# A hybrid-heads decoder layer: small vectors asked for by GpSimd, x scaled on ScalarE in halves, and 14 and 13 pairs visited in the second and third groups

## The chip, the cores and the metric

The kernel runs on one core of one Trainium2 chip. The metric is the device time of one execution in microseconds (us). Three timed runs of the kernel before are known, and one further execution of it was taken with the hardware profiler; all rows below come from that one.

The engines are named as the profile names them: PE is TensorE's matmul, PEld its weight load, DVE is VectorE, ACT is ScalarE, POOL is GpSimd, SP is SyncE, whose queue (SPq) issues the transfers of this kernel.

## What is computed

One decoder layer over 256 tokens and 2048 columns, all in float32. The parts that matter here are the first half: a modulated RMSNorm, one wide projection, and four token mixers that share it.

```python
mod = (cond @ w_mod[l] + b_mod[l]).reshape(B, 6, D)          # cond = silu(c)
sh1, sc1, g1, sh2, sc2, g2 = [mod[:, i, None, :] for i in range(6)]
h = rmsnorm(x, norm_mix[l]) * (1.0 + sc1) + sh1
proj = f32(h @ w_in[l])                                      # 2048 x 5660
y_a = gla_mixer(...)            # needs gla_w_lr, gla_b_lr, gla_norm
y_b = gated_deltanet_mixer(...) # needs gdn_conv, gdn_a_log, gdn_dt_bias, gdn_norm
y_c = pool_mixer(...)           # needs pool_w, pool_scale
y_d = forgetting_attention(...) # needs fox_f_bias
x = x + g1 * (concat(y_a, y_b, y_c, y_d) @ w_out[l])
h = rmsnorm(x, norm_ffn[l]) * (1.0 + sc2) + sh2
x = x + g2 * conv_ffn(h, ...)
```

## The kernel before

**Products in three parts.** Each weight piece (a tile `wr`, 512 KB, loaded by SP) is split into a rounded part `wh` (a cast on ACT, line 115) and a rest `wl` (a subtraction on DVE, line 100), and each product is three matmuls: high by high, high by low, low by high. One loaded piece of `w_in` feeds 24 matmuls of 256 columns. `wr` has 5 buffers, `wh` and `wl` have 3 each.

**Four groups.** The 16 blocks of 128 input columns are taken in four groups of four (`GROUPS`, line 46). For each group, `mods(g)` computes the shift and scale of its columns as a vector product on DVE: 16 tiles `wm` of 512 KB are loaded and added into `ga` one after the other (`accumulate`, lines 168 to 172; `wm` has 5 buffers there). The function `f` inside `mods4` (lines 342 to 354) then folds `ga` with eight tiny matmuls against `ones`, makes `md`, scales the normalized and transposed x (`xnT`, stored in `bigC`) into `h`, and splits `h` into the matmul operand `HL` (stored in `bigA`). Before the first group, x is loaded (`xt`), its squares are summed, GpSimd raises the sum to the power -1/2 (line 320), x is scaled row by row (lines 321 and 322), and 32 transposes on PE with copies on ACT make `xnT`.

**What a group computes.** In stage g, `gdn(g)` (lines 410 to 424) adds the group's part of the DeltaNet's query, key and value into six PSUM tiles `acc` that stay open over all groups: 6 pieces, 144 matmuls. Then `extras(g)` (lines 470 to 474) visits some of the 16 *pairs* of 128-column tiles that make up the rest of the projection (`pairs`, in `ORDER` "gpfd": 6 for GLA, 2 for pooling, 6 for the forgetting attention, 2 for the DeltaNet's gate). A visit (`pair`, lines 438 to 459) multiplies all groups that this pair has not had yet, one piece and 24 matmuls for each, and adds the PSUM tile `ext` into its place (`pr`, `gv` or `fv`). `TAKE` (line 49) says how many pairs stage 0, 1 and 2 visit, counted from the end of the list; the last stage visits all 16. While a stage runs, the loads and additions of the next group's `wm` are interleaved with it (`next(nxt, None)`).

**Small vectors.** `rest()` (lines 367 to 393) loads thirteen small things (the low-rank weights, convolution weights, norms, biases, the constants `ct`), transposes three of them on PE, copies them on ACT, and makes twelve masks `mk` on GpSimd. `small_load()` (lines 396 to 400) loads 28 columns of `w_in` into `wsm` by three transfers of 16, 8 and 4 columns, that is 2048 pieces of 64, 32 and 16 bytes, and splits them into `wsh` (ACT) and `wsl` (DVE). Both are called after the third piece of `gdn(0)`. `small()` multiplies with them at the start of stage 3, and `gates()` follows.

**The last stage and the mixers.** After `gdn(3)`, the accumulators are copied and convolved, and `gated_deltanet()` runs as a long chain of small steps on PE (tiles `gdt`), DVE and ACT. PE fills its gaps with the pairs still to visit (`ext`), with GLA, pooling and forgetting attention (`oxt`), and with the vector products for the second half (`bgt` on PE, more `ga` on DVE). The output projection (`project`, lines 950 to 968, first into `ext`, then into `wot`) follows.

**What sets the order.** A planner orders each engine's instructions by the time at which it expects them to be ready, and by their place in the code where several are. On the chip every engine and every queue then runs its list strictly in that order: an instruction whose input is late holds up all that stand behind it on its engine. `tc.issue_after(x)` puts the instructions of a block behind `x` on the engine of `x`.

Of the kernel before, what the change touches and what calls it, by code (L numbers as in the profile page):

```python
# [11 lines left out]
AF = mybir.ActivationFunctionType  # L12
ALU = mybir.AluOpType
# [32 lines left out]
GROUPS = ((0, 4), (4, 4), (8, 4), (12, 4))  # L46
NG = len(GROUPS)

TAKE = (16, 12, 11)

ORDER = "gpfd"

# [21 lines left out]
def trunk_kernel(ctx: ExitStack, tc: tile.TileContext, x, c, w_mod, b_mod, norm_mix, norm_ffn, w_in,  # L74
# [24 lines left out]
    def tt(o, a, b, op):  # L99
        V.tensor_tensor(out=o, in0=a, in1=b, op=op)  # L100
# [4 lines left out]
    def tsc(o, a, s1, s2, op0, op1=None):  # L105
        if op1 is None:
            V.tensor_scalar(out=o, in0=a, scalar1=s1, scalar2=None, op0=op0)
        else:
            V.tensor_scalar(out=o, in0=a, scalar1=s1, scalar2=s2, op0=op0, op1=op1)

    def act(o, a, f, **kw):
        S_.activation(o, a, f, **kw)

    def split(hi, lo, src):
        S_.copy(hi, src)  # L115
        tt(lo, src, hi.bitcast(F32), ALU.subtract)
# [111 lines left out]
    with ExitStack() as ph:  # L228
# [59 lines left out]
        with ExitStack() as st:  # L288
# [29 lines left out]
                act(flat(pr[:, 0:8]), xt[:, t], AF.Square, accum_out=ssm[:, t:t + 1])  # L318
            tsc(ssm[:, 2:4], ssm[:, 0:2], 1.0 / D, EPS, ALU.mult, ALU.add)
            G.tensor_tensor(out=ssm[:, 0:2], in0=ssm[:, 2:4], in1=mhalf[:, 0:2], op=ALU.pow)  # L320
            for t in range(NT):
                tsc(xt[:, t], xt[:, t], ssm[:, t:t + 1], None, ALU.mult)
            for k in range(0, KT, 2):
                b = ext().rearrange("p (k t) -> p k t", t=T)
                for kk in range(2):
# [9 lines left out]
            def mods(g):  # L335
                for k0 in range(GROUPS[g][0], sum(GROUPS[g]), 4):
                    yield from mods4(k0, min(4, sum(GROUPS[g]) - k0))

            def mods4(k0, nk):
                n = nk * P  # L340

                def f(ga):
                    b = ext()
                    for i in range(2 * nk):
                        mm(b[:, i:i + 1], ga[:, i * P:i * P + P], ones[:, 0:1])
                    md = sp.tile([P, 2 * nk], F32, name="md", tag="md", bufs=2, padded_shape=[P, 16])
                    tt(md[:, 0:nk], b[:, 0:nk], bm(0, k0, nk), ALU.add)
                    tt(md[:, nk:], b[:, nk:2 * nk], bm(1, k0, nk), ALU.add)
                    tt(md[:, nk:], md[:, nk:], nmix[:, k0:k0 + nk], ALU.mult)
                    for kk in range(nk):  # L350
                        k = k0 + kk
                        h = sp.tile([P, T], F32, name="h", tag="h", bufs=2)
                        act(h, xnT[:, k], AF.Identity, scale=md[:, nk + kk:nk + kk + 1], bias=md[:, kk:kk + 1])
                        split(HL[:, k, 0:T], HL[:, k, T:], h)
                views = [wm_v[:, k, 0:2 * D].rearrange("p (s n) -> p s n", n=D)[:, :, P * k0:P * k0 + n]
                         for k in range(KT)]
                ga = keep.tile([P, 2 * n], F32, name="ga", tag="ga", padded_shape=[P, 1024])
                for k in range(KT):
                    wm = sp.tile([P, 2 * n], F32, name="wm", tag="wm", bufs=5, padded_shape=[P, 1024])
                    last_wm[0] = nc.sync.dma_start(wm.rearrange("p (s n) -> p s n", n=n), views[k])  # L360
                    accumulate(ga, wm, k)
                    if k == KT - 1:
                        with tc.high_priority():
                            f(ga)
                    yield

            def rest():
                nc.sync.dma_start(wlr[0:16], gla_w_lr[0])
                nc.sync.dma_start(wlr[28:29], gla_b_lr)
                nc.sync.dma_start(r2[0:48], gdn_conv[0].rearrange("j (k p) -> (j k) p", p=P))  # L370
                nc.sync.dma_start(r2[48:52], pool_scale[0].rearrange("(k p) -> k p", p=P))
                nc.sync.dma_start(r2[52:53], gla_norm)
                nc.sync.dma_start(r2[53:54], gdn_norm)
                nc.sync.dma_start(ct, cst[:, P:K_N])
                row = lambda ap: ap.partition_broadcast(P).rearrange("p o h -> p (o h)")
                nc.sync.dma_start(hrow[:, 0:4], row(gdn_a_log))
                nc.sync.dma_start(hrow[:, 4:8], row(gdn_dt_bias))
                nc.sync.dma_start(hrow[:, 8:12], row(fox_f_bias))
                nc.sync.dma_start(r3, ffn_conv_w[0, 0:2].rearrange("j (k p) -> (j k) p", p=P))
                nc.sync.dma_start(r4[0:NF], ffn_conv_w[0, 2].rearrange("(k p) -> k p", p=P))  # L380
                nc.sync.dma_start(r4[NF:], ffn_conv_b[0].rearrange("(k p) -> k p", p=P))
                b = ext()
                PE.transpose(b[:, 0:54], r2, ident[0:54, 0:54])
                S_.copy(V2, b[:, 0:54])
                b = ext()
                PE.transpose(b[:, 0:2 * NF], r3, ident[:2 * NF, :2 * NF])
                PE.transpose(b[:, 2 * NF:4 * NF], r4, ident[:2 * NF, :2 * NF])
                S_.copy(V3, b[:, 0:3 * NF])
                S_.copy(CB, b[:, 3 * NF:4 * NF])
                S_.copy(idr, ident)  # L390
                S_.copy(ngr, K(K_NEG))
                for i, m_ in enumerate(up + lw):
                    G.tensor_scalar(out=m_, in0=K(K_LV), scalar1=float(i + 1), scalar2=None, op0=ALU.is_equal)


            def small_load():
                nc.sync.dma_start(wsm[:, :, 0:16], wi_v[:, :, C_LR:C_LR + 16])
                nc.sync.dma_start(wsm[:, :, 16:24], wi_v[:, :, C_B:C_B + 8])
                nc.sync.dma_start(wsm[:, :, 24:28], wi_v[:, :, C_FF:C_FF + 4])  # L399
                split(wsh, wsl, wsm)  # L400

            def small():
                o = ext()[0:28, 0:T]
                for k in range(KT):
                    mm(o, wsh[:, k], HL[:, k, 0:T], start=k == 0, stop=False)
                    mm(o, wsh[:, k], HL[:, k, T:], start=False, stop=False)
                    mm(o, wsl[:, k], HL[:, k, 0:T], start=False, stop=k == KT - 1)
                S_.copy(smT[0:28], o)
# [101 lines left out]
            for g in range(NG):  # L510
                nxt = mods(g + 1) if g < NG - 1 else iter(())
                with tc.issue_after(hold[0].ins):
                    if g == NG - 1:
                        small()
                        gates()
                    for i, _ in enumerate(gdn(g)):
                        next(nxt, None)
                        if g == 0 and i == 2:
                            rest()
                            small_load()  # L520
                    if g == NG - 1:
                        break
                    for _ in extras(g):
                        next(nxt, None)
                for _ in nxt:
                    pass
                hold[0] = last_wm[0]


            qc = bigC()  # L530
# [600 lines left out]
```

## Time and profile before

| | us |
|---|---|
| median of 3 runs | 1305.72 (1299.94 to 1308.62) |
| the profiled execution | 1303.01 |
| its span from first to last instruction | 1301.2 |
| PE busy in it | 1248.5 (96%) |
| DVE busy | 891.0 (68%) |
| ACT busy | 636.7 (49%) |

The page of the profile cuts the span into 40 slices of 32.5 us. Busy PE time there does not mean full speed: matmuls overlap, so a stretch is better judged by how many matmuls it held and by the clock that TensorE was granted (PEclk, 1.00 for 2.4 GHz, 0.50 for 1.2 GHz).

### The profile page before, as it was taken

The numbers are of one execution on the slowest core, as the hardware profiler recorded it, in microseconds if no ns is written. First come the engines' busy times: TensorE is split into PE (matmuls) and PEld (weight loads), VectorE is DVE, ScalarE is ACT, GpSimd is POOL, SyncE is SP. The second block draws the span as 40 slices with busy tenths as digits, with TensorE's granted clock in tenths as the row PEclk, the third lists the DMA queues.
The fourth block names the chain that finished last, engine by engine and source line by source line (L and its number), as shares of the span: only waits on it lengthen the run. The fifth ranks groups of instructions, "written<-read, shape, count | busy, mean of one in ns | idle before, by whom it ended". The sixth has DMA issues, their size and how long they took to land.

```text
span 1301.2 us, 20372 instructions
## 1 busy us (share of the span) xinstructions
PE 1248.5 (96%) x7927; PEld 1091.0 (84%) x7927; DVE 891.0 (68%) x1201; ACT 636.7 (49%) x1000; POOL 22.7 (2%) x31
## 2 busy tenths in 40 slices
PE   2799999999999999999999999999999999999996
PEld 1799999898876788888888888888888888888896
DVE  7689797989763397676656656665656597964543
ACT  3455344774354454564545555554555454443432
POOL 0200000010000100000000000000000000000000
PEclk9799999999999999999999999999999999999998
DMA  9999998796566988556576666666665699875652
GB/s 321 277 367 378 337 341 290 259 339 212 164 236 240 318 317 276 156 165 192 163 214 190 186 187 193 190 172 206 187 187 163 219 374 359 323 243 194 192 181 81
DMA packets 174231, 311.94 MB, mean 240 GB/s; under 512 B 16172, under 2 KB 65331, under 8 KB 173495
## 3 DMA queue, kind: packets, MB, share of 16 engines
q1 hardware_dynamic: 174135, 310.65, 72.9%
q8 instruction: 62, 1.02, 0.3%
q14 instruction: 34, 0.28, 0.1%
HBM read 308.51 MB, written 2.10 MB: 239 GB/s over the span
## 4 chain that ended last, share of the span: by engine, by line
PE 92%; DMA 4%; SPq 1%; DVE 1%; ACT 1%; issue 1%; POOLq 0%; ACTq 0%; DVEq 0%
PE fpt L97 57%; PE ext L97 16%; PE wot L97 5%; PE gdt L97 4%; PE acc L97 4%; PE bgt L97 3%; DMA wm<-in_w_mod_dram 3%; PE oxt L97 2%; DMA wr<-in_w_in_dram 1%; DVE ga L103 1%; DMA ct<-in_cst_dram 0%; ACT xT L1011 0%; DVE wl L100 0%; SPq L399 0%; SPq L155 0%
## 5 line engine op out<-in xcount | busy, mean ns | idle before, releaser
L100 DVE TENSOR_TENSOR wl<-wr,wh 128x1024 fp32r<-128x1024 f32 x384 | 469.2, 1223 | 293.6 <-ACT wh L115 292.6
L115 ACT CAST wh<-wr 128x1024 fp32r<-128x1024 f32 x384 | 403.4, 1051 | 494.9 <-PE fpt L97 310.8
L97 PE MATMUL fpt<-bigA,wh 128*128 128x512 f32 x1408 | 399.6, 395 | 2.1 <-DVE bigA L103 2.1
L97 PEld LDWEIGHTS fpt<-bigA,wh 128*128 128x128 f32 x1408 | 239.3, 189 | 32.8 <-issue 2.2
L97 PEld LDWEIGHTS fpt<-bigA,wl 128*128 128x128 f32 x1408 | 222.4, 188 | 34.4 <-DVE wl L100 3.6
L97 PE MATMUL fpt<-bigA,wl 128*128 128x256 f32 x1408 | 240.4, 279 | 0.0
L103 DVE SCALAR_TENSOR_TENSOR ga<-wm,cond,ga 128x1024 f32<-128x1024 f32 x139 | 177.8, 1279 | 9.5 <-DMA wm<-in_w_mod_dram 8.6
L97 PE MATMUL fpt<-wl,AH 128*128 128x512 f32 (+1 forms) x440 | 152.9, 348 | 0.0
L97 PE MATMUL fpt<-wh,AL 128*128 128x512 f32 (+1 forms) x440 | 152.5, 347 | 0.0
L97 PE MATMUL fpt<-wh,AH 128*128 128x512 f32 (+1 forms) x440 | 142.5, 348 | 0.0
L97 PE MATMUL ext<-bigA,wh 128*128 128x256 f32 x768 | 137.0, 280 | 0.0
L97 PEld LDWEIGHTS ext<-bigA,wh 128*128 128x128 f32 x768 | 117.3, 188 | 3.1 <-DVE dS L100 0.8
L97 PE MATMUL ext<-bigA,wl 128*128 128x256 f32 x384 | 107.2, 280 | 1.7 <-DVE wl L100 1.7
L97 PEld LDWEIGHTS fpt<-wh,AH 128*128 128x128 f32 x440 | 83.3, 189 | 10.7 <-issue 0.2
L97 PEld LDWEIGHTS fpt<-wh,AL 128*128 128x128 f32 x440 | 83.3, 189 | 10.5 <-issue 0.2
L97 PEld LDWEIGHTS fpt<-wl,AH 128*128 128x128 f32 x440 | 83.3, 189 | 10.5 <-issue 0.2
L97 PE MATMUL acc<-bigA,wh 128*128 128x256 f32 x384 | 70.3, 289 | 4.7 <-ACT bigA L115 2.9
L97 PEld LDWEIGHTS ext<-bigA,wl 128*128 128x128 f32 x384 | 72.1, 188 | 3.0 <-DVE wl L100 2.1
L97 PE MATMUL ext<-wh,bigA 128*128 128x256 f32 (+1 forms) x320 | 68.0, 304 | 0.0
L97 PEld LDWEIGHTS acc<-bigA,wh 128*128 128x128 f32 x384 | 60.7, 198 | 5.1 <-ACT bigA L115 3.0
L97 PE MATMUL wot<-wh,bigA 128*128 128x512 f32 (+1 forms) x256 | 63.2, 337 | 0.0
L97 PEld LDWEIGHTS ext<-wh,bigA 128*128 128x128 f32 x320 | 51.7, 188 | 5.5 <-ACT wh L115 1.7
(340 smaller groups left out, 1191.9 us busy)
## 6 DMA issues: line engine op xcount, KB each, us to landing
wm<-in_w_mod_dram SPq DMA_DIRECT2D x192, 512.0 KB, 5.8
wr<-in_w_in_dram SPq DMA_DIRECT2D x88, 512.0 KB, 9.7
wr<-in_ffn_w_gate_dram SPq DMA_DIRECT2D x88, 512.0 KB, 3.9
wr<-in_ffn_w_up_dram SPq DMA_DIRECT2D x88, 512.0 KB, 4.4
wr<-in_ffn_w_down_dram SPq DMA_DIRECT2D x88, 512.0 KB, 4.5
wr<-in_w_out_dram SPq DMA_DIRECT2D x32, 512.0 KB, 4.2
xt<-in_x_dram SPq DMA_DIRECT2D x2, 1024.0 KB, 7.2
bigC<-in_x_dram SPq DMA_DIRECT2D x2, 1024.0 KB, 8.6
```

Of the source, the lines that this page charges most:

```text
L97: PE.matmul(o, lhsT=l, rhs=r, start=start, stop=stop, skip_group_check=True)
L100: V.tensor_tensor(out=o, in0=a, in1=b, op=op)
L103: V.scalar_tensor_tensor(out=o, in0=a, scalar=s, in1=b, op0=op0, op1=op1)
L115: S_.copy(hi, src)
```

## The change

Four edits. (1) x is scaled on ACT instead of DVE, in two halves of 1024 columns for each of the two row tiles. (2) The thirteen small transfers and the three of `wsm` are issued by GpSimd instead of SP. They stand behind a multiplication that GpSimd now does for group 1 (`asked`), `wsm` first. (3) The work on them moves back: `rest()` (transposes, copies, masks) is called after stage 2, and the split of `wsm` stands in `small()`. (4) `TAKE` is (16, 14, 13) instead of (16, 12, 11).

```diff
-TAKE = (16, 12, 11)
+TAKE = (16, 14, 13)
...
-            for t in range(NT):
-                tsc(xt[:, t], xt[:, t], ssm[:, t:t + 1], None, ALU.mult)
+            for hs in (slice(0, D // 2), slice(D // 2, D)):
+                for t in range(NT):
+                    act(xt[:, t, hs], xt[:, t, hs], AF.Copy, scale=ssm[:, t:t + 1])
...
+            asked = [None]
...
-                    tt(md[:, nk:], md[:, nk:], nmix[:, k0:k0 + nk], ALU.mult)
+                    if k0 == GROUPS[1][0]:
+
+                        asked[0] = G.tensor_tensor(out=md[:, nk:], in0=md[:, nk:], in1=nmix[:, k0:k0 + nk], op=ALU.mult)
+                    else:
+                        tt(md[:, nk:], md[:, nk:], nmix[:, k0:k0 + nk], ALU.mult)
...
+            def rest_load():
+                G.dma_start(wlr[0:16], gla_w_lr[0])
...
+                G.dma_start(ct, cst[:, P:K_N])
...
+                G.dma_start(hrow[:, 0:4], row(gdn_a_log))
...
+                G.dma_start(r4[NF:], ffn_conv_b[0].rearrange("(k p) -> k p", p=P))
+
             def rest():
-                nc.sync.dma_start(wlr[0:16], gla_w_lr[0])
...
-                nc.sync.dma_start(r4[NF:], ffn_conv_b[0].rearrange("(k p) -> k p", p=P))
                 b = ext()
                 PE.transpose(b[:, 0:54], r2, ident[0:54, 0:54])
...
             def small_load():
-                nc.sync.dma_start(wsm[:, :, 0:16], wi_v[:, :, C_LR:C_LR + 16])
-                nc.sync.dma_start(wsm[:, :, 16:24], wi_v[:, :, C_B:C_B + 8])
-                nc.sync.dma_start(wsm[:, :, 24:28], wi_v[:, :, C_FF:C_FF + 4])
+                for o, c, n in ((0, C_LR, 16), (16, C_B, 8), (24, C_FF, 4)):
+                    G.dma_start(wsm[:, :, o:o + n], wi_v[:, :, c:c + n])
+
+            def small():
                 split(wsh, wsl, wsm)
-
-            def small():
...
                         next(nxt, None)
-                        if g == 0 and i == 2:
-                            rest()
-                            small_load()
...
                 hold[0] = last_wm[0]
+                if g == 0:
+                    with tc.issue_after(asked[0].ins):
+                        small_load()
+                        rest_load()
+                if g == 2:
+                    rest()
```

What this does to the lists of the engines shows at three places. The first is SP's list in stage 0. Before, the end of the small transfers stands between the pieces of the first two `gdn(0)` steps and the next ones:

```order
L374 DMA ct<-in_cst_dram 128x960
L376 DMA hrow<-in_gdn_a_log_dram 128x4
L377 DMA hrow<-in_gdn_dt_bias_dram 128x4
L378 DMA hrow<-in_fox_f_bias_dram 128x4
L379 DMA r_112<-in_ffn_conv_w_dram 88x128
L380 DMA r_113<-in_ffn_conv_w_dram 44x128
L381 DMA r_113<-in_ffn_conv_b_dram 44x128
L397 DMA wsm<-in_w_in_dram 128x16x16
L398 DMA wsm<-in_w_in_dram 128x16x8
L399 DMA wsm<-in_w_in_dram 128x16x4
L155 DMA wr<-in_w_in_dram 128x2x512
L360 DMA wm<-in_w_mod_dram 128x2x512
```

In the change SP's list goes straight on, from the last 16 `wm` of group 0 on:

```order
L367 DMA wm<-in_w_mod_dram 128x2x512 x16
L155 DMA wr<-in_w_in_dram 128x2x512 x3
L367 DMA wm<-in_w_mod_dram 128x2x512
L155 DMA wr<-in_w_in_dram 128x2x512 x2
L367 DMA wm<-in_w_mod_dram 128x2x512 x4
L155 DMA wr<-in_w_in_dram 128x2x512
L155 DMA wr<-in_w_in_dram 128x4x256 x2
L367 DMA wm<-in_w_mod_dram 128x2x512 x5
```

No small transfer is left between them, and the three `wr` behind the sixteenth `wm` follow each other.

The second place is ACT's list at the end of stage 0 in the change, where the cast of `wsm` now stands (`fv` and `pr` take the last pairs of stage 0; the `wh` behind `wsh` are the second to fifth piece of `gdn(1)`):

```order
L438 COPY fv<-ext 128x2x256
L115 CAST wh<-wr 128x1024
L438 COPY pr<-ext 128x512 x2
L115 CAST wsh<-wsm 128x448
L115 CAST wh<-wr 128x1024 x4
L400 CAST ngr<-ct 128x128
L112 ACT_TABLE_LOAD
L112 ACTIVATE ea<-hrow 128x4
L115 CAST wh<-wr 128x1024 x14
```

Before, that cast stood between the split of `h` of group 0 and the fourth piece of `gdn(0)`:

```order
L115 CAST bigA<-h 128x256 x2
L115 CAST wsh<-wsm 128x448
L115 CAST wh<-wr 128x1024 x2
```

So it moved back by one whole stage, but it still stands among the casts that feed PE, with `ngr` and `ea` (which need `ct` and `hrow`) four casts behind it.

The third place is PE's list at the end of the DeltaNet. Before, its last products (`gdt<-bigC,dI` and what follows, second row tile), the transposes of the first row tile's result `Y`, and then the output projection (`ext<-wh,bigA`):

```order
L97 MATMUL gdt<-bigC,dI 128x128 x4
L97 MATMUL gdt<-dS,bigC 64x128 x4
L97 MATMUL gdt<-X,bigC 64x128 x4
L873 MATMUL oxt<-ident,p 128x128
L97 MATMUL bgt<-ga,ones 128x512
L97 MATMUL oxt<-pr 128x256
L97 MATMUL oxt<-ct,la 128x256
L97 MATMUL oxt<-ct,la 128x128
L97 MATMUL oxt<-ngr,idr 128x128
L735 MATMUL gdt<-ident,Y 128x128 x4
L97 MATMUL ext<-wh,bigA 128x512 x2
L97 MATMUL ext<-wl,bigA 128x512
```

In the change, the same products, and then the transposes of both row tiles at once:

```order
L97 MATMUL gdt<-bigC,dI 128x128 x4
L97 MATMUL gdt<-dS,bigC 64x128 x4
L97 MATMUL gdt<-X,bigC 64x128 x4
L746 MATMUL gdt<-ident,Y 128x128 x8
L97 MATMUL wot<-wh,bigA 128x512
L97 MATMUL wot<-wl,bigA 128x512
```

The first three quarters of that output projection piece stand ahead of these products now, and nothing stands between the last product and the transposes.

## Rows read from the trace of the kernel before

**Rows 1.** Page, parts 1 and 2: busy us (share) xcount; 40 slices in tenths.
```profile
PE 1248.5 (96%) x7927; PEld 1091.0 (84%) x7927; DVE 891.0 (68%) x1201; ACT 636.7 (49%) x1000; POOL 22.7 (2%) x31
PE   2799999999999999999999999999999999999996
PEclk9799999999999999999999999999999999999998
```
**Rows 2.** Stretches: us from:to length, busy us (xcount) by engine, PEclk, DMA share, GB/s.
```profile
10.00:18.00 8.00, 2.67 (x10) 1.64 (x10) 6.29 (x9) 2.14 (x5) 0.70 (x1) 1.00 1.05 384
18.00:26.00 8.00, 4.57 (x24) 3.40 (x24) 7.79 (x7) 4.08 (x7) 0.00 (x0) 1.00 0.90 271
42.00:52.00 10.00, 9.84 (x63) 9.51 (x64) 4.02 (x7) 3.89 (x10) 6.52 (x12) 0.72 0.61 80
42.00:80.00 38.00, 33.88 (x252) 32.98 (x253) 24.94 (x25) 16.23 (x26) 6.52 (x12) 0.88 0.94 290
42.00:48.00 6.00, 5.83 (x27) 5.51 (x28) 4.02 (x7) 3.89 (x10) 3.05 (x6) 0.54 0.60 110
58.00:62.00 4.00, 4.00 (x24) 4.00 (x23) 2.88 (x3) 2.17 (x4) 0.00 (x0) 0.61 1.06 385
100.00:120.00 20.00, 20.00 (x176) 20.00 (x175) 18.81 (x19) 12.51 (x20) 0.00 (x0) 1.00 1.06 380
120.00:140.00 20.00, 18.31 (x162) 18.12 (x161) 16.58 (x16) 7.56 (x8) 0.00 (x0) 1.00 1.07 370
240.00:380.00 140.00, 139.75 (x1141) 123.53 (x1140) 116.32 (x183) 75.18 (x147) 6.74 (x4) 1.00 0.71 239
380.00:440.00 60.00, 59.69 (x386) 35.97 (x385) 24.12 (x69) 27.96 (x74) 0.00 (x0) 1.00 0.76 256
```
**Rows 3.** The chain that ended last, in order of time: start us, us, what.
```profile
21.52 5.92 DMA wm<-in_w_mod_dram
...
40.04 4.65 DMA ct<-in_cst_dram
...
46.55 2.71 SPq L399
```
**Rows 4.** Timeline, 10 to 60 us: DVE's x scaling and additions, SP's small transfers, ACT's `wsh`.
```profile
13.86 2.48 DVE L107 TENSOR_SCALAR xt<-xt,ssm 128x2048 f32<-128x2048 f32 x2
16.25 10.52 DVE L103 SCALAR_TENSOR_TENSOR ga<-wm,cond,ga 128x1024 f32<-128x1024 f32 x8
...
39.77 0.22 SPq L373 DMA_DIRECT2D r<-in_gdn_norm_dram  x1
...
44.02 0.40 SPq L397 DMA_DIRECT2D wsm<-in_w_in_dram  x1
...
49.30 1.12 SPq L155 DMA_DIRECT2D wr<-in_w_in_dram  x1
...
52.34 0.57 ACT L115 CAST wsh<-wsm 128x448 fp32r<-128x448 f32 x1 [5.19 <-DMA wsm<-in_w_in_dram]
```
**Rows 5.** Groups of instructions, 100 to 220 us: busy us, mean ns, idle before.
```profile
L100 DVE TENSOR_TENSOR wl<-wr,wh 128x1024 fp32r<-128x1024 f32 x42 | 51.0, 1218 | 4.7 <-ACT wh L115 4.2
L103 DVE SCALAR_TENSOR_TENSOR ga<-wm,cond,ga 128x1024 f32<-128x1024 f32 x30 | 38.4, 1279 | 0.1
L100 DVE TENSOR_TENSOR pr<-ext,pr 128x512 f32<-128x512 f32 x15 | 10.3, 686 | 5.7 <-PE ext L97 5.6
```
**Rows 6.** Timeline of PE, ACT and POOL at the end of the DeltaNet, 440 to 458 us.
```profile
440.09 1.09 PE L97 MATMUL gdt<-dS,bigC 128*64 128x128 f32 x8
...
444.42 1.14 ACT L112 ACTIVATE Y<-gdt,oss 128x128 f32<-128x128 f32 x4 [1.77 <-DVE oss L100]
...
451.56 1.85 POOL L726 TENSOR_TENSOR oss<-oss,mhalf 128x4 f32<-128x4 f32 x1 [7.37 <-DVE oss L109]
```
**Rows 7.** Groups of POOL's instructions over the whole span: busy us, mean ns.
```profile
L393 POOL TENSOR_SCALAR mk<-ct 128x128 uint8<-128x128 f32 x12 | 6.5, 549 | 32.7 <-DMA ct<-in_cst_dram 32.1
L320 POOL TENSOR_TENSOR ssm<-ssm,mhalf 128x2 f32<-128x2 f32 x1 | 0.7, 697 | 11.5 <-DVE ssm L109 11.5
```

More of the change, by code (lines that the diff above doesn't have):

```diff
@@ L365, in mods4 @@
                     yield
-            def rest():
-                nc.sync.dma_start(wlr[0:16], gla_w_lr[0])
[L369 to L380, printed above, removed]
-                nc.sync.dma_start(r4[NF:], ffn_conv_b[0].rearrange("(k p) -> k p", p=P))
+            def rest_load():
+                G.dma_start(wlr[0:16], gla_w_lr[0])
+                G.dma_start(wlr[28:29], gla_b_lr)
+                G.dma_start(r2[0:48], gdn_conv[0].rearrange("j (k p) -> (j k) p", p=P))
+                G.dma_start(r2[48:52], pool_scale[0].rearrange("(k p) -> k p", p=P))
+                G.dma_start(r2[52:53], gla_norm)
+                G.dma_start(r2[53:54], gdn_norm)
+                G.dma_start(ct, cst[:, P:K_N])
+                row = lambda ap: ap.partition_broadcast(P).rearrange("p o h -> p (o h)")
+                G.dma_start(hrow[:, 0:4], row(gdn_a_log))
+                G.dma_start(hrow[:, 4:8], row(gdn_dt_bias))
+                G.dma_start(hrow[:, 8:12], row(fox_f_bias))
+                G.dma_start(r3, ffn_conv_w[0, 0:2].rearrange("j (k p) -> (j k) p", p=P))
+                G.dma_start(r4[0:NF], ffn_conv_w[0, 2].rearrange("(k p) -> k p", p=P))
+                G.dma_start(r4[NF:], ffn_conv_b[0].rearrange("(k p) -> k p", p=P))
+            def rest():
                 b = ext()
```

## The prediction

> **What bounds the kernel now.** I read the page's engine totals and slices first: PE is busy 96% of the span, and apart from the first two slices and the last it is at 9 in every one, DVE at 68%, ACT at 49% [rows 1]. A busy PE need not be a full one, so next the table of stretches. In 100:120 PE held 176 matmuls in 20 us at clock 1.00 [rows 2], 0.1136 us each; a weight piece of 24 takes 2.73 us. In stages 0 to 2 nothing else limits so tightly, though DVE and the transfers come close: DVE 18.8 of the 20 us, DMA share 1.06 at 380 GB/s [rows 2]. So an edit counts by the PE time that it frees or adds. Before about 80 us the PE is not filled, and there I looked with the chain of waits and the timeline [rows 3, 4].
>
> **The start: x scaled on ACT.** DVE scales x from 13.86 for 2.48 us, and behind that stand eight additions of `ga`, 10.52 us without a gap [rows 4]. Each frees a `wm` buffer; the chain shows the `wm` transfer of 21.52 among what ended last [rows 3]. The loss is visible in the transfers: 384 GB/s in 10:18, 271 in 18:26 [rows 2]. Of 8 us at about 380 that is (380 - 271) x 8 / 380 = 2.3 us of transfer time. With the scaling on ACT the additions start up to 2.48 us sooner. I take 2.2 us gained; the bounds are 0 (the stream is limited elsewhere) and 2.5. ACT's four scalings of 1024 columns lie under the additions: their inputs exist at 13.86, `md` needs `ga` only some 10 us later, and ACT had 4.1 busy us of the 8 in 18:26 [rows 2]. Without that cover they would cost about what DVE's two did.
>
> **The gap in SP's queue.** SP spends 39.77 to 49.30 on small transfers, before the next `wr` is issued, 9.5 us [rows 4]; the chain goes through `ct` and the last of `wsm` [rows 3]. In 42:52 the transfers move 80 GB/s [rows 2]. In 42:80 PE does 252 matmuls, 28.6 us at full speed, in 38 us: 9.4 lost [rows 2]. Of these, 42:48 at clock 0.54 loses 6 x 0.46 = 2.8 us; that is the climb after the idle start, and stays. The clock falls again in 58:62 (0.61, 1.6 us), after PE had run short of weights, and the other 5.0 us are waits. With pieces following each other on SP's queue, a 512 KB piece takes 1.4 us at 380 GB/s against 2.73 us of PE. So I take the 6.6 us as gained; bounds 0 and 6.6.
>
> What it does not remove is the transfers' own work. At share 0.61 of 10 us, that is about 6 us of the sixteen engines; it returns in stage 1, where the share is already 1.06 [rows 2]. The Trainium skill ("DMA: Bandwidth & Descriptors", section "Issuing engines are not separate DMA queues") says that transfers issued by different engines run on the same 16 DMA engines and interleave, and that only the sequencer's time to start them is saved. By it the 9.5 us of SP's time are saved and the engines' work is not; that is the third rival, and the trace of before, with all on SP, cannot show it.
>
> **Two more visits in stages 1 and 2.** Each of these stages takes two pieces from the last stage: 4 x 24 = 96 matmuls, 10.9 us of PE, moved and not added. A visit costs DVE one `wl` (1.218) and one addition of `pr` (0.686) [rows 5], 1.9 us under 2.73 us of PE; there are four more additions in all, 2.7 us of DVE, hidden. Stage 1 gets looser: 18 pieces are 49.1 us of PE, and DVE has 18 x 1.218 + 16 x 1.279 + 12 x 0.686 = 50.6 us, the transfers 34 x 1.38 = 46.9. With 20 pieces PE has 54.6, DVE 54.4, transfers 49.7. In 120:140 PE did 162 instead of 176, 1.6 us lost [rows 2]. With transfers that are further ahead I take these 1.6 as gained; bounds 0, and 5.3 for the whole of 100:220 (42 pieces, x42 in [rows 5], are 114.7 us of the 120).
>
> **What the moved visits no longer cover.** In 240:380 PE loses nothing, but in 380:440 weight loads are busy only 36 of 60 us with 386 matmuls [rows 2]: the mixers' own chain, with pairs as filler. The order of the change shows the cost at one place: the last DeltaNet products are followed at once by the transposes of `Y`. For the first row tile, products ended at 441.18 and `Y` was done at 445.56 [rows 6], 4.4 us that PE spent on the out-projection. GpSimd's power inside it took 1.85 us in the other tile [rows 6], and one addition of 1.28 us may stand in DVE's list between the steps. I take 5 us lost; bounds 0 (the filler ahead lets the products finish when their inputs arrive, so the gap was there anyway) and 8.
>
> **The rest.** GpSimd's multiplication for group 1 takes about its `ssm` product's 0.70 us [rows 7], on a path with six visits of PE queued, so nothing. The masks, 6.5 us of POOL [rows 7], the transposes and copies of `rest()` move behind stage 2, 100 us before their use: nothing; were they late, GLA's first steps would wait up to 7 us.
>
> **The sum.** 1303.0 (the profiled execution) - 2.2 - 6.6 - 1.6 + 5 = 1297.6. That execution was 2.7 below the median of the runs, so on their scale it is 1300.
>
> **The rivals.**
>
> *`wsm` comes late (slower).* ACT's list has the cast of `wsm` right behind the last copies of stage 0 and ahead of the casts for four pieces of `gdn(1)`. GpSimd asks for it only after the multiplication for group 1, some six visits (16 us of PE) earlier. If it lands later, ACT stops, then DVE and PE, us for us. Through SP the landing took 8.3 us, 44.02 to 52.34, on almost idle transfer engines, and ACT had waited 5.19 us for it then [rows 4]. From above: 6144 pieces over 16 engines are 384 each, and if each takes turns with a 2 KB piece of the other queue (380 / 16 = 24 GB/s, 0.087 us) that is 33 us. If GpSimd had to make each piece as it makes a mask column (549 ns for 128 [rows 7], 4.3 ns), 26 us. Between these I put the landing at 12 to 16 us, nearer the SP row, since it is the same transfer on the same engines. At 21 us the rest of the gain (5.4) is gone; at 34 us PE stands 18 us: 1300 + 18 = 1318. `ct` and `hrow` come four casts later, so up to some 15 us more are possible: 1335.
>
> *PE waits for the mixers' chain all along 380:440.* The 10.9 us of filler are missing there and come back as waits, with the tail's: 1300 + 6 = 1306, up to 1312 with the whole 10.9, and 1320 if the clock drops too (0.61 for some 20 us). For it: 36 busy us of weight loads in 60. Against it: there are still out-projection pieces and `bgt`.
>
> *No net gain from the queue.* The small pieces slow the stream in stage 1 by the 6 us they cost in stage 0: 1300 + 5 = 1305. For it: share 1.06. Against it: stage 1 gets 2 x 2.73 us more PE work for 2 x 1.38 of transfer.
>
> *More than the sum.* The tail is covered (0) and stage 1 gives the whole 5.3: 1300 - 5 - 3.7 = 1291. For it: stages 1 and 2 become PE-bound by the sums above.
>
> The Trainium skill ("SBUF — State Buffer", box "The 'DVE blocks DMA' trap") says that GpSimd cannot write its transfers' descriptors while DVE runs a two-port operation. Of that kind DVE would have only a short one per stage here, so by it the first rival would be worse by an us or so; no run here shows it yet.
>
> **How the numbers follow.** Forecast 0.42 (own range 1291 to 1306), `wsm` late 0.22 (1302 to 1335), mixers exposed 0.12 (1304 to 1320), no net gain 0.12 (1303 to 1307), more than the sum 0.12 (1286 to 1292). 1288 to 1318 leaves out about 0.05 below and 0.13 above. One per cent is 13 us, about what a measurement of this kernel can tell from no change: faster is below 1292.7, slower above 1318.8. Faster: the last case and a quarter of the forecast's, 0.22. Slower: three fifths of the first rival and two fifths of the second, 0.18. Same: 0.60.
>
> **What would show it.** Start right: the eight additions begin near 14 and 18:26 moves over 350 GB/s. Queue right: no stretch under 300 GB/s in 42:80, no second clock drop, some 58 matmuls more there. Visits right: 120:140 holds 176. Tail right: PE idles 3 to 8 us before `gdt<-ident,Y`; wrong if it is under 1 or the loss lies before the last products. First rival: a wait of ACT for `wsm` in front of `wsh`, with PE idle behind it and the clock down. Third: DMA share over 1 and GB/s under 350 in the 40 us in which `wsm` and `ct` travel. What would make it wrong above all is a landing of `wsm` over 20 us after its request.

## The result: slower, by 0.45%

The changed kernel took 1309.74 us (median of 12 runs, 1306.13 to 1312.74), the kernel before 1303.95 us beside it (12 runs). The ratio is 1.0045 with a 95% interval of 1.0032 to 1.0059: 5.8 us slower, clear of noise, where 1300 and a small gain were forecast. The time lies inside the whole range that was named (1288 to 1318), but outside the forecast's own range (1291 to 1306) and on the wrong side of the kernel before.

The profiled execution of the changed kernel took 1309.04 us, its span 1307.3. The totals and slices of its page, for [rows 1]:

```profile
PE 1255.0 (96%) x7927; PEld 1091.0 (83%) x7927; DVE 891.9 (68%) x1202; ACT 641.9 (49%) x1004; POOL 40.3 (3%) x48
...
PE   2999999999999989999999999999999999999996
...
PEclk9899999999999989999999999999999999999998
```

The second slice and the climb at the start are better than before. In their place stands a new dip in slice 15 (455 to 490 us), in PE and in the clock. The stretches that answer [rows 2] (us from:to, length, busy us (xcount) of PE, PEld, DVE, ACT, POOL, PEclk, DMA share, GB/s):

```profile
18.00:26.00 8.00, 4.92 (x23) 3.79 (x21) 7.62 (x6) 3.51 (x6) 0.00 (x0) 1.00 1.05 387
42.00:48.00 6.00, 6.00 (x46) 6.00 (x46) 5.55 (x5) 2.04 (x2) 0.00 (x0) 0.84 1.07 372
42.00:80.00 38.00, 38.00 (x319) 37.86 (x319) 31.92 (x27) 17.07 (x20) 0.00 (x0) 0.98 1.07 370
58.00:62.00 4.00, 4.00 (x36) 4.00 (x35) 3.52 (x3) 2.03 (x3) 0.00 (x0) 1.00 1.09 372
80.00:100.00 20.00, 20.00 (x175) 20.00 (x174) 15.42 (x19) 13.14 (x22) 7.91 (x11) 1.00 1.08 308
100.00:120.00 20.00, 18.99 (x162) 18.42 (x161) 16.51 (x14) 9.25 (x12) 16.08 (x18) 1.00 1.05 367
120.00:140.00 20.00, 19.41 (x164) 19.03 (x163) 16.34 (x17) 7.37 (x7) 0.00 (x0) 1.00 1.08 366
380.00:440.00 60.00, 58.62 (x373) 38.98 (x372) 26.78 (x59) 30.32 (x73) 0.00 (x0) 0.97 0.81 276
```

The front did what was forecast: 387 GB/s in 18:26 instead of 271, 319 matmuls in 42:80 instead of 252, no second clock drop. In 80:100 the transfers fall to 308 GB/s, and 100:120 and 120:140 hold 162 and 164 matmuls where the kernel before had 176 and 162. The requests by GpSimd show in POOL's and ACT's timelines:

```profile
88.14 0.57 POOL L354 TENSOR_TENSOR md<-md,V 128x4 f32<-128x4 f32 x1 [75.60 <-DVE md L100]
88.69 3.73 POOL L407 DMA_DIRECT2D wsm<-in_w_in_dram  x3
...
100.42 0.54 POOL L383 DMA_DIRECT2D hrow<-in_gdn_a_log_dram  x1 [0.58 <-DMA wsm<-in_w_in_dram]
...
105.78 13.49 POOL L402 TENSOR_SCALAR mk<-ct 128x128 uint8<-128x128 f32 x12 [2.21 <-DMA ct<-in_cst_dram]
```

```profile
105.11 0.57 ACT L115 CAST wsh<-wsm 128x448 fp32r<-128x448 f32 x1
105.89 1.05 ACT L115 CAST wh<-wr 128x1024 fp32r<-128x1024 f32 x1 [0.21 <-DMA wr<-in_w_in_dram]
109.68 1.05 ACT L115 CAST wh<-wr 128x1024 fp32r<-128x1024 f32 x1 [2.74 <-DMA wr<-in_w_in_dram]
```

`wsm` was there 11.7 us after the first of its three requests (88.69 to 100.42, where the wait for it ends), and its cast waited for nothing; what ACT waits for behind it is the weight pieces `wr`. The last row of POOL's shows that the masks did not move behind stage 2, although `rest()` stands there in the code: POOL's list has them right behind the requests, at 105.78. The three transposes of `rest()` ran at 222 to 225 us.

Two marks divide the time: the last of the `acc` matmuls (end of `gdn(3)`) and the first transposes of the second half of the layer (`fpt<-ident,bigC`). The rows give duration min/median/max in ns, then first and last start. Before:

```profile
L97 PE MATMUL acc<-bigA,wl x192: 276/280/420, 44.4 to 239.5; 128*128 128x256 f32 x192
L1010 PE MATMUL fpt<-ident,bigC x32: 271/273/273, 542.2 to 545.6; 128*128 128x128 f32 x32
```

After:

```profile
L97 PE MATMUL acc<-bigA,wl x192: 276/276/415, 40.2 to 243.1; 128*128 128x256 f32 x192
L1021 PE MATMUL fpt<-ident,bigC x32: 272/273/273, 548.0 to 551.3; 128*128 128x128 f32 x32
```

At 243.1 the changed kernel has done 10.9 us more of pairs than before at 239.5, so the front gained 239.5 + 10.9 - 243.1 = 7.3 us. The rest of the first half took 304.9 us with 10.9 us less to do, against 302.7: 13.1 us lost. The second half of the layer takes the same time in both (759.0 and 759.3 us). So the question is what cost 13 us between 243 and 548, of which 5 were forecast.

### The profile page after: what moved, and what is told of

The parts are those of the page before. It is cut to its first block, busy times and chain, and to the rows that moved or that the text cites. A ratio compares the mean times of both kernels' runs of the same rounds, so it can differ in the third digit from the quotient of the medians.

```text
span 1307.3 us, 20403 instructions
## 1 busy us (share of the span) xinstructions
PE 1255.0 (96%) x7927; PEld 1091.0 (83%) x7927; DVE 891.9 (68%) x1202; ACT 641.9 (49%) x1004; POOL 40.3 (3%) x48
## 4 chain that ended last, share of the span: by engine, by line
PE 86%; DMA 7%; DVE 3%; ACT 1%; issue 1%; SPq 0%; POOLq 0%; ACTq 0%; DVEq 0%
PE fpt L97 57%; PE ext L97 12%; DMA wm<-in_w_mod_dram 4%; PE wot L97 4%; PE gdt L97 4%; PE bgt L97 3%; PE acc L97 3%; DMA wr<-in_w_in_dram 3%; DVE ga L103 2%; PE oxt L97 2%; ACT wh L115 0%; DVE wl L100 0%; ACT xT L1022 0%; ACT bigC L112 0%; PE oxt L884 0%
## 5 line engine op out<-in xcount | busy, mean ns | idle before, releaser
L100 DVE TENSOR_TENSOR wl<-wr,wh 128x1024 fp32r<-128x1024 f32 x384 | 469.1, 1223 | 301.5 <-ACT wh L115 300.3
```

## The experiments

In this table the two marks are those of each kernel's one profiled execution, so a difference of 3 us in the last three columns says little: e3 and e12, whose PE list in the last stage is the same, differ by 3.4 in the last one. The last stage is the time between them plus the 10.9 us (or 5.5 for TAKE (16, 13, 12)) that the moved visits take out of it. Ratios are to the kernel before, run on the same chip; differences in the text go by the ratios, unless medians are named.

| kernel | median us | ratio (95%) | end of gdn(3) | second half starts | last stage |
|---|---|---|---|---|---|
| before | 1302.5 to 1304.0 | 1 | 239.5 | 542.2 | 302.7 |
| changed | 1309.74 | 1.0045 (1.0032 to 1.0059) | 243.1 | 548.0 | 315.8 |
| e1: TAKE set back | 1303.56 | 1.0007 (0.9993 to 1.0020) | 232.9 | 541.5 | 308.6 |
| e2: TAKE alone | 1318.86 | 1.0122 (1.0103 to 1.0140) | 249.3 | 557.2 | 318.8 |
| e3: x on ACT alone | 1299.92 | 0.9974 (0.9961 to 0.9987) | 233.3 | 538.7 | 305.4 |
| e4: requests and their work alone | 1306.55 | 1.0024 (1.0010 to 1.0039) | 233.7 | 545.1 | 311.4 |
| e5: only the work moved | 1309.81 | 1.0046 (1.0024 to 1.0068) | 237.5 | 548.8 | 311.3 |
| e6: e1 with rest() after stage 1 | 1295.49 | 0.9951 (0.9937 to 0.9965) | 234.1 | 536.9 | 302.8 |
| e7: TAKE (16, 13, 12) | 1299.46 | 0.9978 (0.9966 to 0.9990) | 236.3 | 537.7 | 306.9 |
| e8: changed, rest() after stage 1 | 1312.20 | 1.0076 (1.0057 to 1.0095) | 242.4 | 549.1 | 317.6 |
| e9: e7 with rest() after stage 1 | 1300.92 | 0.9986 (0.9974 to 0.9998) | 235.9 | 540.3 | 309.9 |
| e10: changed, projection held back | 1307.71 | 1.0033 (1.0022 to 1.0044) | 243.0 | 548.9 | 316.8 |
| e11: e6, requests a stage later | 1301.43 | 0.9983 (0.9969 to 0.9997) | 237.5 | 539.0 | 301.5 |
| e12: e6, wsm in one transfer (twelve other columns) | 1293.69 | 0.9921 (0.9903 to 0.9939) | 229.8 | 531.8 | 302.0 |

**The parts of the change, one at a time.** The first four kernels put edits back or in alone: e1 is the change with `TAKE = (16, 12, 11)`, e2 the kernel before with `TAKE = (16, 14, 13)`, e3 the kernel before with the scaling on ACT, e4 the kernel before with edits 2 and 3.

```diff
-TAKE = (16, 14, 13)
+TAKE = (16, 12, 11)
```

> The changed kernel with TAKE set back to (16, 12, 11); the other three edits stay. Theory A: in the change's trace PE reaches the end of gdn(3) at 243.4 us where the kernel before has 239.8, with 96 matmuls (10.9 us) more done by then, so the front gained about 7.3 us, and the last stage, from there to the first FFN product, lost about 13 us by the two visits moved per stage. Then this kernel keeps the 7.3 and loses nothing: 1304 - 7.3 = 1296.7, ratio 0.994, and its output projection interleaves with the last DeltaNet products as before. Rival B: the front's lead is given back later whatever TAKE is, since the mixers' chain or the transfers of the last stage come at their own time; then this kernel takes 1303 to 1310.

> The kernel before with TAKE set to (16, 14, 13) and nothing else. Theory A: the last stage loses about 13 us, less at most 1.6 us that looser stages 1 and 2 give: 1304 + 11 to 13 = 1315 to 1317, ratio 1.009 to 1.010, with PE idle twice around the transposes of Y. Rival B: the loss of the last stage comes from the moved requests and rest(), not from the visits; then this kernel takes 1302 to 1305.

> The kernel before with the scaling of x on ACT in halves and nothing else. Predicted gain 2.2 us: 1301.8, ratio 0.998; the transfers in 18:26 rise from 271 to over 350 GB/s. Rival: the gain is caught by the gap in SP's queue at 40 us, which then comes 2 us sooner and ends 2 us sooner too (still 1302), or the half-clock climb starts sooner but ends at the same matmul (1304, ratio 1.000).

> The kernel before with the small transfers issued by GpSimd and their work moved back (edits 2 and 3), x still scaled on DVE, TAKE (16, 12, 11). Theory A: 7.3 us less the 2.2 of the scaling, so -5.1: 1299, ratio 0.996; no stretch under 300 GB/s in 42:80, and about 1.4 us of PE given back in 80:140 while wsm and ct travel. Rival C (the small pieces take from the stream in stage 1 all that they cost in stage 0): 1303 to 1304, with 6 us of PE missing in 80:140.

Theory A, that the loss is all in the visits, fell. e3 gained 3.4 us as forecast, or a little more. e2 lost 15.9 us where 11 to 13 were expected. But e4 lost 3.1 us where a gain of 5 was expected, and e1 was no faster than the kernel before: both end `gdn(3)` some 6 us early, and give it back in the last stage (311.4 and 308.6 us against 302.7), without any visit moved. So there are two causes in the last stage. The rows of 352 to 372 us, of before, e4 and e1, show where one of them is to be seen:

```profile
352.00:372.00 20.00, 20.00 (x150) 15.34 (x149) 12.35 (x22) 12.21 (x37) 2.02 (x2) 1.00 0.68 233
```

```profile
352.00:372.00 20.00, 20.00 (x122) 15.81 (x119) 9.77 (x17) 10.35 (x28) 1.01 (x1) 0.83 0.55 185
```

```profile
352.00:372.00 20.00, 20.00 (x124) 16.43 (x125) 11.31 (x21) 9.03 (x30) 2.01 (x2) 0.83 0.42 144
```

The granted clock falls there to 0.83 on the mean, part of the stretch at the lower of its two levels (1.2 of 2.4 GHz), 3.4 us lost. PE counts as busy throughout, so nothing but the clock and the 26 to 28 missing matmuls tells it. (e4 has two such stretches more in 262:302, where its mean clock is 0.91; e1 has none there, which is enough for the difference between their last stages.)

**Requests or work?** e4 differs from the kernel before in who asks, and in when the work on the small vectors is done. That work stands in PE's list only as a few transposes, but the planner orders all that follows by it: PE's order in the last stage is not the same. e5 leaves the requests with SP and moves the work alone (the split of `wsm` into `small()`, too); e6 leaves the requests with GpSimd and calls `rest()` one stage earlier, after which PE's order in the last stage is that of the kernel before again. The third, e7, halves the moved visits.

```diff
 # e5, to the kernel before
...
-                            rest()
+                            rest_load()
                             small_load()
...
                 hold[0] = last_wm[0]
+                if g == 2:
+                    rest()
```

```diff
 # e6, to the change with TAKE (16, 12, 11)
-                if g == 2:
+                if g == 1:
                     rest()
```

> The kernel before with only the work on the small vectors moved back: SP still asks for them in stage 0, but rest() is called after stage 2 and the split of wsm stands in small(). PE's order in the last stage is then that of the run with requests by GpSimd, and not that of before. Theory M (the moved work, by the order that it leaves in the last stage, costs there): 240 to 395 us takes 3 to 4 us more of waiting than in the kernel before, and some clock on top: 1302.5 + 3 to 6 = 1306 to 1309, ratio 1.002 to 1.005. Rival Q (the requests by GpSimd and their transfers cost, the work does not): 1301 to 1303, ratio 1.000.

> The changed kernel with TAKE (16, 12, 11) and rest() called after stage 1 in place of stage 2; PE's order in the last stage is then nearly that of the kernel before. Theory M: the 3.6 us of waiting and the extra clock losses of the last stage go, and what is left is the gain of the scaling and about 0.5 us of the requests: 1302.5 - 4 = 1298.5, ratio 0.997, and gdn(3) ends near 233 us as with rest() after stage 2. Rival Q: as with rest() after stage 2, 1303 to 1304, ratio 1.000 to 1.001.

> The changed kernel with TAKE (16, 13, 12), that is with half of the moved visits. If the loss by TAKE is the filler that is missing, piece by piece, half of the 6.2 us between TAKE (16, 12, 11) and (16, 14, 13) with the other edits: 1303.4 + 3 = 1306.5, ratio 1.003. If it is the order that tips over at one point (the last DeltaNet products with or without out-projection behind them), it is all or nothing: 1303 to 1304 with products between the last DeltaNet products and the transposes of Y, or 1309 to 1310 without.

Theory M held on both sides. The moved work alone costs 6.0 us (e5), in a kernel where GpSimd asks for nothing; and with the requests by GpSimd but the old order of PE, e6 is 0.5% under the kernel before, 3 us faster than expected, with a last stage of 302.8 us. The traces let PE's lists be compared instruction by instruction, by operation and tile, from the last `acc` to the first `fpt<-ident,bigC`: the list of e6 is the one of before, and e1, e4 and e5 share another, from which it differs at some 430 of 2084 places. So the three kernels with the slower list have last stages of 308.6 to 311.4 us, whoever asks, and the two with the old one 302.7 and 302.8. DVE's, ACT's and SP's lists change along with PE's, so which engine's order costs is not separated. In e5 the clock falls at the same place, in e6 it doesn't:

```profile
352.00:372.00 20.00, 20.00 (x124) 15.53 (x124) 11.94 (x21) 8.25 (x20) 1.01 (x1) 0.83 0.56 185
```

```profile
352.00:372.00 20.00, 20.00 (x158) 16.89 (x158) 11.62 (x19) 11.60 (x35) 2.01 (x2) 1.00 0.75 251
```

How much is clock can be estimated from all runs, since each lists its span and mean granted clock: (1 - clock) x span, on the mean over the runs, is 16.6 us for e6 and 20.4 for e1, and the span without it 1277.7 and 1281.2. So of the 7 us between them about half is clock, and half is not.

e7 agreed with neither case: 1299.46 us, by the medians 4.1 faster than e1 though it moves two visits more than e1. The loss by TAKE is no price per visit.

**The visits.** e8 asks whether the two causes add up, e9 whether moving `rest()` always helps. e10 tests the term of the prediction that named the hole at the transposes of `Y`: two pieces of the output projection are held behind the last DeltaNet product.

```diff
 # e10, to the changed kernel; final[0] is the last DeltaNet product
...
-                for kk, k, t in steps:
...
+                with (tc.issue_after(final[0].ins) if n == 0 and j in (4, 5) else ExitStack()):
+                    for kk, k, t in steps:
...
```

> The changed kernel with rest() called after stage 1 in place of stage 2, TAKE (16, 14, 13) as changed. PE's order is then nearly that of the run with TAKE alone (16.4 us slower than the kernel before). If the effects of the front and of PE's order in the last stage add up: 1303 + 16.4 - 7.7 = 1312, ratio 1.007, slower than the changed kernel although the same move of rest() made the kernel with TAKE (16, 12, 11) 8 us faster. Rival: rest() after stage 2 has a price of its own, whatever the order, and this kernel takes 1302 to 1303.

> The changed kernel with TAKE (16, 13, 12) and rest() called after stage 1. If the loss by the moved work belongs to the order at TAKE (16, 12, 11) alone: 1299, ratio 0.997, as with rest() after stage 2. If moving rest() back always costs its 6 us: 1293, ratio 0.992, and this would be the fastest kernel so far (1295.5 with TAKE (16, 12, 11) and rest() after stage 1).

> The changed kernel, with the fifth and sixth piece of the first output projection (24 matmuls, 5.5 us, from the forgetting attention's columns) held behind the last DeltaNet product, so that they stand between it and the transposes of Y; all else is in the order of the change. Theory T (the hole at the transposes is a matter of what stands in it): the two idle stretches of 2.4 and 2.0 us, and most of the half-clock time behind them (1.9 and 1.5 us lost), go: 1309.7 - 5 to 7 = 1303 to 1305, ratio 0.996 of the changed kernel, about 1.000 of the kernel before; the last product ends some 5 us sooner. Rival H (the DeltaNet's chain itself is late): the products wait for their inputs, PE idles ahead of them in place of behind, and the time stays at 1308 to 1310.

e8 took 1312.2 us, the 1312 of the sum: with TAKE (16, 14, 13) the earlier `rest()` gives exactly PE's list of e2 in the last stage, which is the worse one (317.6 and 318.8 us, against 315.8 in the changed kernel), and the same move that won 7 us at TAKE (16, 12, 11) loses 4. e9 stayed within 1.5 us of e7. So it is neither the place of `rest()` nor the number of visits by itself; the last stage goes with the order that the planner makes of both.

The hole at `Y` is in the change's trace as it was predicted. PE, end of the DeltaNet, and the stretch around it (90 matmuls at clock 1.00 before, without idle time):

```profile
463.83 0.71 PE L97 MATMUL gdt<-X,bigC 128*64 128x128 f32 x5
466.98 1.00 PE L746 MATMUL gdt<-ident,Y 128*128 128x128 f32 x4 [2.44 <-ACT Y L112]
470.01 1.25 PE L746 MATMUL gdt<-ident,Y 128*128 128x128 f32 x4 [2.04 <-ACT Y L112]
```

```profile
460.00:480.00 20.00, 15.53 (x76) 12.32 (x75) 14.43 (x21) 9.03 (x31) 2.97 (x2) 0.83 0.90 324
```

That is 4.5 us of idle time and 3.4 us of clock, more than half of the 13.1 lost. But e10 won 2.0 us by the medians (1.6 by the ratios, whose intervals overlap) where 5 to 7 were expected. It filled half of the hole: the first transposes no longer wait, the second ones still do. And PE now stands ahead of the last products, waiting for a cast, with the clock down behind it. These are e10's rows (the changed kernel has 58.62 busy us in 380:440):

```profile
380.00:440.00 60.00, 55.96 (x366) 36.01 (x364) 25.16 (x58) 28.92 (x72) 0.00 (x0) 0.98 0.79 265
440.00:460.00 20.00, 19.96 (x90) 15.57 (x90) 12.80 (x21) 8.95 (x15) 0.95 (x1) 0.87 0.76 272
```

```profile
438.81 1.22 PE L97 MATMUL ext<-wh,bigA 128*128 128x512 f32 x2 [2.25 <-ACT wh L115]
473.08 0.63 PE L747 MATMUL gdt<-ident,Y 128*128 128x128 f32 x4 [2.52 <-ACT Y L112]
```

By time rival H was nearer. Its reason, that the products wait for their own inputs, is not shown: what PE waits for at 438.81 is a weight. So it stays open how much of the loss the hole causes, and how much it only takes up.

The order gives a hint where cover was lost earlier. The rows of `ext` alone (PE, PEld, DVE, ACT, PEclk, DMA share, GB/s) in 350:380 show it, for the kernel before, e6, e7, e2 and the changed kernel:

```profile
350.00:380.00 30.00, 11.19 (x85) 10.09 (x84) 2.07 (x3) 0.00 (x0) 1.00 0.49 167
```

```profile
350.00:380.00 30.00, 10.06 (x73) 8.96 (x73) 2.75 (x4) 0.00 (x0) 1.00 0.57 189
```

```profile
350.00:380.00 30.00, 5.85 (x35) 4.66 (x35) 1.38 (x2) 0.00 (x0) 1.00 0.47 148
```

```profile
350.00:380.00 30.00, 2.27 (x18) 1.86 (x16) 1.37 (x2) 0.00 (x0) 0.94 0.51 167
```

```profile
350.00:380.00 30.00, 0.47 (x5) 0.27 (x3) 0.69 (x1) 0.00 (x0) 1.00 0.61 202
```

The pairs are PE's cover for the mixers' small products. Before, they last to 380 us; in the changed kernel they are gone at 350, and what is left to put between the products are the vector products `bgt`, which need `wm` pieces. Its chain shows such a piece on its way:

```profile
363.37 1.92 PE bgt L97 x16
365.29 6.61 DMA wm<-in_w_mod_dram
371.94 1.05 PE bgt L97 x4
```

PE worked through most of those 6.61 us and stood for 0.57 and 0.17 us of them, and for 1.34 us more at 401.50; the kernel before has such a piece later in its chain (3.94 us at 381.49) and stood 0.31 us for it. Where fewer pairs are left in 350:380, the last stage is longer in the main, but no run put pairs back there alone: that the missing cover is the cause is not shown.

**What the requests cost in the stream.** e11 asks a stage later, e12 asks for `wsm` with fewer, larger pieces; both are e6 otherwise. e12 leaves out that twelve of the 28 columns lie elsewhere in `w_in`, so it doesn't compute this layer and serves for its time alone.

```diff
 # e11
-                    if k0 == GROUPS[1][0]:
+                    if k0 == GROUPS[2][0]:
...
-                if g == 0:
+                if g == 1:
                     with tc.issue_after(asked[0].ins):
```

```diff
 # e12
-                for o, c, n in ((0, C_LR, 16), (16, C_B, 8), (24, C_FF, 4)):
-                    G.dma_start(wsm[:, :, o:o + n], wi_v[:, :, c:c + n])
+                G.dma_start(wsm, wi_v[:, :, C_LR:C_LR + 28])
```

> The kernel with TAKE (16, 12, 11) and rest() after stage 1, with the requests a stage later: behind the multiplication for group 2, near 157 us in place of 87, where the transfers have slack (DMA share 0.91 to 1.03 in 140:200 against 1.04 to 1.08 in 80:140). Theory D (the requests cost in 100:140 because the weight stream has no slack there: 137 and 164 matmuls against 174 and 179 with the old requests, 5.9 us): that comes back in 100:140, little is lost later, and the time is 1295.5 - 3 to 5 = 1291 to 1293, ratio 0.992. Rival L (wsm lands 12 us after its request, and its cast stands some 12 to 15 us behind the multiplication): ACT waits for wsm near 170 us, PE loses there what it won, 1295 to 1298.

> The kernel with TAKE (16, 12, 11) and rest() after stage 1, with wsm asked for by one transfer of 2048 pieces of 112 bytes in place of three with 6144 pieces of 64, 32 and 16 bytes. It takes 28 neighbouring columns, so the twelve for beta, decay and forget gate hold other columns of w_in; the work on them is the same. If the small pieces are what costs in 80:140: two thirds of their part, 100:140 rises from 301 to 320 or more matmuls, and the time falls by 2 to 3 us to 1293, ratio 0.993. If it is the bytes, ct and the order of landing: 1295 to 1296 and about 301 matmuls.

The 16 us with most of the requests (they run from 87 to 102 us in e6), in e3 (no requests there), e6 and e12:

```profile
84.00:100.00 16.00, 16.00 (x140) 15.87 (x139) 13.56 (x17) 10.89 (x18) 0.00 (x0) 1.00 1.08 367
```

```profile
84.00:100.00 16.00, 16.00 (x140) 16.00 (x139) 12.97 (x16) 11.04 (x19) 8.86 (x13) 1.00 1.08 288
```

```profile
84.00:100.00 16.00, 16.00 (x140) 16.00 (x139) 13.50 (x17) 11.86 (x20) 9.50 (x17) 1.00 1.07 344
```

The transfer engines are as busy in all three, and move 367, 288 and 344 GB/s. As an estimate, the small transfers take (367 - 288) x 16 / 367 = 3.4 us of the stream in e6 and 1.0 us in e12, and the pieces of `wsm`, fewer and larger in e12, make the difference. PE feels it afterwards. These are 42:80 and 100:140 of e3, then of e6:

```profile
42.00:80.00 38.00, 35.49 (x278) 34.74 (x278) 24.66 (x23) 15.24 (x22) 6.22 (x12) 0.94 1.01 315
100.00:140.00 40.00, 39.83 (x350) 39.64 (x349) 35.49 (x33) 17.14 (x21) 0.00 (x0) 1.00 1.07 375
```

```profile
42.00:80.00 38.00, 38.00 (x328) 37.98 (x328) 32.97 (x28) 17.99 (x21) 0.00 (x0) 0.99 1.07 370
100.00:140.00 40.00, 35.89 (x298) 34.67 (x297) 31.35 (x29) 15.28 (x18) 11.20 (x17) 1.00 1.06 363
```

What e6 wins over e3 in the first stretch, 50 matmuls, it loses in the second, 52. e12 holds 329 in 100:140. It took 1.8 us less than e6 by the medians, which are of different chips, and 3.9 by the ratios; 2 to 3 were expected. e11 went against its theory: 100:140 is clean (342 matmuls), but behind the later requests the `wm` pieces come late. An addition of `ga` waits for one, the addition of `pr` behind it in DVE's list comes late, and PE stands, with the clock at 0.83 in 180:200:

```profile
184.11 0.80 PE L97 MATMUL ext<-bigA,wh 128*128 128x256 f32 x2 [6.13 <-DVE pr L100]
```

e11 is 4.2 us slower than e6, so a DMA share a little under 1 was no slack here.

## Why the prediction was wrong, point by point

Put together by the ratios, the change is: scaling on ACT -3.4 us (e3), requests by GpSimd -3.0 (e3 to e6), their work moved behind stage 2 +7.3 (e6 to e1), two more visits in stages 1 and 2 +5.0 (e1 to the change). These are steps from one kernel to the next, so their sum must come out (+5.9, against 5.8 measured), and the price of a step depends on the ones taken before it: the visits alone cost 15.9 us (e2). The prediction had -2.2, -6.6, 0 and -1.6 + 5.

- **The start** was right, and somewhat larger: the additions run on from 12.60 us with no scaling between them, 18:26 moves 387 GB/s, and the whole is 3.4 us. By the end of `gdn(3)` it is even 6.2 (239.5 to 233.3), of which e3's last stage gives 2.7 back.
- **The gap in SP's queue** was seen rightly, and its signs came (42:80 gained 67 matmuls, more than the 58 named, and the second clock drop is gone), but the term of 6.6 us was too large. By the end of `gdn(3)`, the requests with their work bring 5.8 us alone (e4) and the scaling 6.2 alone (e3), but both together 5.4 to 6.6 (e6, e1): with the scaling done, the front gains next to nothing more. So there the rival "No net gain from the queue" held, and its sign, under 350 GB/s at a share over 1, is in 80:100. The 3.0 us of e6 lie behind the front, in a last stage whose order of PE is not that of e3, and by the estimate above in the clock: (1 - clock) x span is 19.4 us in e3 and 16.6 in e6; what brings them is not shown. The Trainium skill ("DMA: Bandwidth & Descriptors", section "Issuing engines are not separate DMA queues") says just this, that the transfers share the same 16 engines whoever issues them; the trace agrees, with 288 instead of 367 GB/s at the same share of 1.08.
- **"The masks, 6.5 us of POOL [rows 7], the transposes and copies of `rest()` move behind stage 2, 100 us before their use: nothing"** is the step that failed. The masks were done by 119.3 us and the transposes ran 18 us before the end of `gdn(3)`, so nothing came late. The move cost 7.3 us all the same (e6 to e1; 6.0 in e5), because the planner places other instructions by it, and the order of the last stage came out another way. The prediction read that order only at the tail.
- **The tail** was there as predicted: 4.5 us idle, inside the 3 to 8 named and near the 5 taken, and half clock behind it, which the sum did not have. That the two more visits in each stage cost 5.0 us from e1 to the change is luck in part: alone they cost 15.9, and in between, at TAKE (16, 13, 12), there is a gain. Whether the loss belongs to this one place is not settled, since e10 filled only half of it. The rival *PE waits for the mixers' chain all along* is seen in part, with 1.34 us idle in 380:440 and a mean clock of 0.97 there.
- **The 1.6 us of 120:140** did not come: 162 matmuls before, 164 after. The looser stage gave nothing there: with TAKE alone (e2) the stretch holds 159, while with the scaling alone (e3) it holds 179. In e6, with the requests but TAKE (16, 12, 11), it holds 164 again.
- **`wsm` late**, the rival on the slower side, did not happen: it landed 11.7 us after the request, just under the 12 to 16 taken, and ACT did not wait. The largest part of the loss, that of the moved work, no rival named.

A version that beats both: e6, the change with TAKE left at (16, 12, 11) and `rest()` after stage 1, 1295.5 us, 0.5% under the kernel before and 0.9% under the changed one by the ratios.

What stays open: which single swap in PE's last stage brings the clock down at 352 to 372 us in e1, e4 and e5. That it goes with the order, and not with the requests, is shown by e5 and e6. The other half of that loss is no idle time: in 240:380 PE is busy 139.56 us in e1 and 139.16 in e6, but does 1081 and 1133 matmuls; it was not traced further. Open, too, is which part of the 5.0 us of the visits the hole at `Y` causes.

## What to carry to other kernels

Where a planner sets the order, an instruction that is moved under full cover need not be free: compare the order of the stage that is short of cover, not only the place that the instruction left. Work that fills a late stage's gaps is worth more there than in an early stage that is full anyway, so moving it forward needs the row that shows what will stand in the gaps. And edits that remove the same idle time don't add up (6.2 and 5.8 us alone, 5.4 to 6.6 together): price the second with the first already done.

## What the runs showed of the hardware

- Small pieces cost transfer time when GpSimd issues them, too. With 6144 pieces of 16 to 64 bytes for `wsm` the stream moved 288 instead of 367 GB/s for 16 us, 3.4 us of it; with 2048 of 112 bytes, 344 GB/s and 1.0 us (estimates; the thirteen other small transfers are in both).
- GpSimd's requests are not free for GpSimd: three for `wsm` took 3.73 us and others about 0.5 us each. The ninth waited for a `wsm` to land (2.9 us in the changed kernel, 4.1 in e12); in the changed kernel the next two did as well (0.9 us, and the 0.58 before the row at 100.42 above), the later ones no more.
- The twelve masks took 13.49 us in the changed kernel, 9.58 in e6 and 6.5 before [rows 7]. Their single rows show with what it goes. These are two masks of the changed kernel, and the DVE addition that runs when the second starts:

```profile
109.98 0.53 POOL L402 TENSOR_SCALAR mk<-ct 128x128 uint8<-128x128 f32 x1
112.44 1.17 POOL L402 TENSOR_SCALAR mk<-ct 128x128 uint8<-128x128 f32 x1
111.91 1.31 DVE L103 SCALAR_TENSOR_TENSOR ga<-wm,cond,ga 128x1024 f32<-128x1024 f32 x1
```

  No DVE instruction runs when the first starts. The second ends 0.39 us after the addition does. All nine slow ones end 0.38 to 0.41 us after the addition or subtraction under which they started, and the three others take 0.52 to 0.53 us.
- The mean granted clock explains much of the spread between runs of some kernels: e1's spans range over 10.7 us (1296.4 to 1307.1), and over 4.6 us (1278.7 to 1283.3) without the clock's loss. In e7 it explains none (4.0 us, and 5.6 without it).
